# Sample attention units moved by half a stage in a one-core decoder-trunk kernel, with the block of the new values last in each unit's sum

## The chip, the core and the metric

The kernel runs on one core of one Trainium2 chip, as one program. The metric is the device time of one execution in microseconds (us); lower is better. Before the change it is 2066.39 us, the median of 3 runs (2065.44 to 2069.13).

## The reference

One inference step of a small decoder trunk, on a prompt of 512 tokens and on 8 samples of 8 new tokens each, in float32, width 1024. Layer 1 is a convolution module and a gated feed-forward block (FFN). Layer 2 is attention with 16 heads of 64 in three dilation groups (windows 128, 512 and 2048, dilations 1, 4 and 16) and another FFN. Keys and values are shared between the groups' queries as in the lines below; the samples attend to a cache of 1024 earlier rows and to their own new rows.

```python
h, st = conv_module(x, ...);  x = x + h                    # layer 1
x = x + swiglu(x, ...)
k, v = shared_kv(x, pos, kv_norm, w_kv, k_norm)            # layer 2: 3 groups, 16 heads
q = queries(x, pos, b_norm, w_q, q_norm)
for g in range(3):                                         # prompt: band_attention
    kg, vg, valid = gather_keys(cache_g, k[:, :, g], v[:, :, g], r_g, W_g // r_g)
    o_g, lse_g = gathered_attention(q[:, :, g], kg, vg, valid)      # samples
x = x + merge_groups(outs, lses, w_o)                      # softmax over the groups' lse
x = x + swiglu(x, ...)
```

## The kernel before

The work runs in this order: convolution layer, FFN 0, attention, merge (the projection with `w_o`), FFN 1. Two blocks of the convolution are done on VectorE. Every float32 product of the projections is three TensorE matmuls (`mm3`, lines 228 to 230) on operands that ScalarE and VectorE split into a high and a low half. TensorE is busy almost without a break outside the attention.

The attention has two parts.

*The projection stages.* `stage(s)` for s = 0 to 3 computes queries, keys and values of four heads (256 columns, `CW`) in 9 chunks: kind 0 (queries), 1 (keys), 2 (values), each for three dilation groups g. A chunk is a generator with 5 yields, so a stage has 45 steps. At the yields the weight slice `whi`, `wlo` for a later chunk is loaded (`wraw`, 1024 KB) and split. Queries and keys are normed and rotated; the samples' part of them is put into `Qz[s % 2]` and `KN[s]` by `new_keys`, five ticks (about one chunk) after its chunk. Finished rows go to DRAM: `scr` for the prompt, `scs` for the samples' new keys and values, both by `store`, also five ticks later.

*The prompt phase.* `prompt()` does the band attention of the 512 prompt tokens, two heads at a time (8 pairs p), in 88 steps. Per pair it reads back three `nat` tiles of 512 KB (queries and keys), three `v` tiles of 256 KB, and exchanges softmax statistics through DRAM (`sx`, `ot`, `scc`, `cb`).

*The samples' attention* is cut into 8 units u; unit u serves stage s = u // 2 and four of the eight samples. It has steps at whole numbers i relative to its base step 12 + 32 u (`LEAD + u * PERIOD + i`):

- i = -12 to 12: nine loads of old keys, tile `kk` (512 KB each, five buffers; some are issued as two halves);
- i = 0 to 25: TensorE transposes of these tiles into `tp` (line 964), copied by ScalarE to `kt`;
- i = 14, 26, 29: scores, TensorE on `tp` (line 989), the last of them with `KN[s]`, and VectorE's masked maximum; i = 31 to 33 the exponentials;
- i = 33 to 55: ten loads of values, tile `vv` (four buffers), each 8 steps ahead of its use: nine of 512 KB from the cache, and one (ti = 1) of three small transfers from `scs`, the new values;
- i = 37 to 43: transposes of the probabilities; i = 41 to 63: the sum over ten value blocks in the PSUM tile `pv` (line 1062); i = 65 to 67: the result goes to `as`.

Call i up to 31 the first half of a unit and i from 32 the second half. The units overlap: the second half of u runs beside the first half of u + 1, 32 steps later. There are 304 sample steps in all.

`weave` merges two generators: it always runs the one that is behind in its share, so both end together. Before, stage 0 is woven with 33 empty steps and then 12 sample steps, the stages 1 to 3 with 64 sample steps each (`WIN`), and the prompt phase with the 100 that are left.

All these DMAs are issued by one queue, SyncE's (SP), in program order. The order is written out by hand in this sense: the instructions stand on each engine as the woven generators emit them.

Of the kernel before, what the change touches and what calls it, by code (L numbers as in the profile page):

```python
# [90 lines left out]
def trunk(ctx: ExitStack, tc: tile.TileContext, I, O, dbg=None):  # L91
    nc = tc.nc
# [778 lines left out]
    def attention(as_):  # L871
# [26 lines left out]
        def rows2(b, kind, c0):  # L898
            return ck[1][b, :, kind, c0:c0 + CW].rearrange("(j p) c -> p j c", p=128)

        def load3(t, b, kind, c0, q0, q1):
            v = ck[2][b, :, kind, c0:c0 + CW].rearrange("(j q t) c -> t j q c", q=8, t=2)
            for i in range(2):
                nc.sync.dma_start(t[64 * i:64 * i + 64], v[i, :, q0:q1])

        def kk():
            return sm.tile([128, 4, CW], F32, tag="kk", name="kk", bufs=5)

        KN = {}
        PERIOD, LEAD = 32, 12  # L910
        WIN = (64, 64, 64)
        steps = {}

# [16 lines left out]
        pvt = sps.tile([128, CW], F32, name="pv")  # L930

        def sample_unit(u):
# [5 lines left out]
            def at(i, order=1):  # L938
                def put(f):
                    steps.setdefault(LEAD + u * PERIOD + i, []).append((order, f))  # L940
                    return f
                return put


            for n in range(9):
                g, bi = (1 + n // 4, n % 4) if n < 8 else (0, 0)
                b = 4 * ub + bi

                @at(3 * n - 12, 2)
                def _(n=n, g=g, b=b):  # L950
                    t = Z["k", n] = kk()
                    if g == 0:
                        nc.sync.dma_start(t, ck[0][4 * ub:4 * ub + 4, :, 0, c0:c0 + CW].rearrange("b p c -> p b c"))
                    elif g == 1:
                        nc.sync.dma_start(t, rows2(b, 0, c0))
                    else:
                        load3(t, b, 0, c0, 0, 4)
# [74 lines left out]
                        nc.scalar.activation(ph[:w, a:z], pt[:w, a - tl[0]:z - tl[0]], AF.Copy)  # L1032


            for ti in range(10):
                t0 = 41 + 5 * ti // 2

                @at(t0 - 8, 2)
                def _(ti=ti):
                    v = Z["v", ti] = sm.tile([128, 4, CW], F32, tag="vv", name="vv", bufs=4)  # L1040
                    bs = slice(4 * ub, 4 * ub + 4)
                    if ti == 0:
                        nc.sync.dma_start(v, ck[0][bs, :, 1, c0:c0 + CW].rearrange("b p c -> p b c"))
                    elif ti == 1:
                        for g in range(G):
                            nc.sync.dma_start(v[T * g:T * g + T], scs[2][g][32 * ub:32 * ub + 32, c0:c0 + CW]
                                              .rearrange("(b t) c -> t b c", t=T))
                    elif ti < 6:
                        nc.sync.dma_start(v, ck[1][bs, 128 * (ti - 2):128 * (ti - 1), 1, c0:c0 + CW]
                                          .rearrange("b p c -> p b c"))  # L1050
                    else:
                        vb = ck[2][bs, :, 1, c0:c0 + CW].rearrange("b (j q t) c -> t q j b c", q=8, t=2)
                        for t in range(2):
                            nc.sync.dma_start(v[64 * t:64 * t + 64], vb[t, ti - 6])

                @at(t0, 0)
                def _(ti=ti):
                    ph, v = Z["ph"], Z.pop(("v", ti))
                    n = 24 if ti == 1 else 128
                    for bi in range(4):  # L1060
                        r = slice(32 * bi, 32 * bi + 32)
                        nc.tensor.matmul(pvt[r], ph[:n, ti, r], v[:n, bi], start=ti == 0, stop=ti == 9)  # L1062

            @at(65, 0)
            def _():
# [19 lines left out]
        NSAMPLE = max(steps) + 1  # L1085

        def sample_steps():
            for i in range(NSAMPLE):
                for _, f in sorted(steps.get(i, []), key=lambda x: x[0]):
                    f()  # L1090
                yield


        def weave(*gens):

            live = [[g, n, 0] for g, n in gens]
            while live:
                live.sort(key=lambda x: (x[2] + 1) / x[1])
                x = live[0]
                try:  # L1100
                    next(x[0])
                    x[2] += 1
                except StopIteration:
                    live.remove(x)
# [16 lines left out]
        def nat_load(p, g):  # L1121

            t = NAT[p, g] = pnat.tile([128, 8, 128], F32, tag="nat", name="nat", bufs=2)
            nc.sync.dma_start(t, scr[g, :2, :, :, p * 128:p * 128 + 128].rearrange("k r j c -> j (k r) c"))

        with xp:
# [116 lines left out]
            def stage(s):  # L1243
                for kind in range(3):
                    for g in range(G):
                        yield from chunk(s, kind, g)
# [5 lines left out]
                                  scs[kind][g].rearrange("(b t) c -> b t c", t=T))  # L1252

            samples = sample_steps()
            def first_loads():
                yield from range(45 - LEAD)
                yield from islice(samples, LEAD)

            weave((stage(0), 45), (first_loads(), 45))
            for s in range(1, NSTAGE):  # L1260
                if s == NSTAGE - 1:
                    for g in range(2):
# [7 lines left out]
        with ExitStack() as px:  # L1270
# [12 lines left out]
            def both(m):  # L1283

                return (2 * m, 2 * m + 1)

            def nat_transpose(p, i):
                g, k = divmod(i, 2)
                t = NAT[p, g][:, 4 * k:4 * k + 4]
                pt = ps.tile([128, 512], F32, tag="tpp", name="tpp", bufs=2)  # L1290
                for r in range(4):
                    x = pt[:, r * 128:(r + 1) * 128]
                    if g == 0:

                        x = pt.rearrange("p (i r jj) -> p r i jj", i=4, r=4)[:, r]
                    nc.tensor.transpose(x, t[:, r], ident)
                d = QK[p, k, g] = pa.tile([128, 512], F32, tag="qk", name="qk", bufs=6)
                nc.scalar.activation(d, pt, AF.Copy)
# [50 lines left out]
            def do_exp(n):  # L1349
                p, lay, e, j = unit(n)  # L1350
                nb, P = NBS.pop(n), PP[n]
                for ii in range(2):
                    c = cols_of(n, ii)
                    nc.scalar.activation(P[:, ii, c], P[:, ii, c], AF.Exp, scale=SC, bias=nb[:, ii:ii + 1],
                                         accum_out=ST[p][:, lay, 2 * j + ii, e, 1:2])
# [92 lines left out]
            NM = NU // 2  # L1448

            def prompt():  # L1450
                for i in range(5):
                    yield
                for i in range(2):
                    nat_transpose(0, i)
                nat_load(0, 2)
                yield
                for m in range(NM + 9):
                    p, k = divmod(m, 4)
                    if 0 <= m - 1 < NM:
                        for n in both(m - 1):  # L1460
                            do_max(n)
                    if 0 <= m - 3 < NM:
                        do_values(m - 3)
                    yield
                    if 0 <= m - 2 < NM:
                        for n in both(m - 2):
                            do_transpose(n)
                    if m < NM:
                        do_scores(m)
                    if 0 <= m - 1 < NM:  # L1470
                        for n in both(m - 1):
                            do_exp(n)

                    q = p + k // 2
                    if k < 3 and q < NP:
                        for i in (2 * k + 2, 2 * k + 3) if k < 2 else (0, 1):
                            nat_transpose(q, i)
                    if k < 3 and p + 1 < NP:
                        nat_load(p + 1, k)
                    if p < NP:  # L1480
                        if k == 0:
                            v_load(p, 0)
                        elif k == 2:
                            v_load(p, 1)
                            v_load(p, 2)
                        elif k == 3 and 1 <= p < 4:
                            new_rows(1, p - 1)
                            new_rows(2, p - 1)
                    for d, f in ((5, exchange), (6, exchanged), (8, coefficients), (9, coefficients_out), (10, coefficients_in),
                                 (12, combine)):  # L1490
                        if (m - d) % 4 == 0 and 0 <= (m - d) // 4 < NP:
                            f((m - d) // 4)
                    yield

            weave((prompt(), 2 * NM + 24), (samples, NSAMPLE - LEAD - sum(WIN)))
        cx.close()
        return ap

# [97 lines left out]
```

## Time and profile before

| | |
|---|---|
| median of 3 runs | 2066.39 us (2065.44 to 2069.13) |
| profiled execution: its time, its span | 2061.0 us, 2059.1 us |
| mean granted TensorE clock | 0.98 |
| busy: TensorE, VectorE, ScalarE, GpSimd | 1950.8, 1013.1, 810.7, 159.9 us |
| DMA | 387.81 MB, 188 GB/s on average |

"PE" is TensorE's matmuls, "PEld" its weight loads, "DVE" VectorE, "ACT" ScalarE, "POOL" GpSimd, "SPq" the issue of DMAs on SP. A table of windows gives for each stretch of time its length, each engine's busy time with the number of instructions, the granted TensorE clock (1.00 is full), the mean busy share of the core's 16 DMA engines, and the GB/s that they moved. Times in a timeline or a chain are microseconds from the start of the span.

### The profile page before, as it was taken

The page shows a single profiled execution, that of the slowest core. Times are in us where ns is not written, and L with a number is a line of the kernel's source. Part 1 is how long each engine was busy: PE and PEld are TensorE (multiplying, and loading weights), DVE is VectorE, ACT ScalarE, POOL GpSimd, SP SyncE. Part 2 cuts the span into 40 slices and gives each one's busy share as a digit, 9 for nine tenths or more (in the row PEclk, how much of TensorE's full clock was granted, in tenths as well). Part 3 has the DMA queues.
Part 4 walks back from the last instruction along what each step waited for, and adds up shares of the span by engine and source line. Part 5 has one row for each costly group of instructions (what it writes and reads, how often), then busy time and mean ns, then how long its engine had stood idle before and what let it go on. Part 6 is the DMA issues. An engine that isn't in the chain of part 4 may idle for free.

```text
span 2059.1 us, 40751 instructions
## 1 busy us (share of the span) xinstructions
PE 1950.8 (95%) x17109; PEld 1801.3 (87%) x17109; DVE 1013.1 (49%) x1922; ACT 810.7 (39%) x1836; POOL 159.9 (8%) x292
## 2 busy tenths in 40 slices
PE   6989799999999999999999999988897999999999
PEld 6767499999999999998888888866566999999998
DVE  5776665432444486564455356325454454324432
ACT  6554633221222343444344344266564332112221
POOL 1000000000000033130122032000112000000000
PEclk9999899999999999999999999989898999999999
DMA  7430196568655856759778887699979555643222
GB/s 211 144 143 22 34 322 224 197 213 292 204 197 189 290 165 198 212 171 259 209 212 230 246 230 211 205 227 220 205 160 249 202 203 197 217 117 82 76 71 75
DMA packets 368873, 387.81 MB, mean 188 GB/s; under 512 B 17983, under 2 KB 357975, under 8 KB 367010
## 3 DMA queue, kind: packets, MB, share of 16 engines
q1 hardware_dynamic: 368130, 384.06, 62.4%
q8 instruction: 135, 2.21, 0.5%
q0 software_dynamic: 560, 1.14, 0.2%
q14 instruction: 48, 0.39, 0.1%
HBM read 348.07 MB, written 146.86 MB: 240 GB/s over the span
## 4 chain that ended last, share of the span: by engine, by line
PE 84%; DMA 6%; ACT 5%; DVE 3%; SPq 1%; issue 1%; another core or an unknown queue 0%; ACTq 0%; DVEq 0%
PE pmm L230 13%; PE pmm L229 13%; PE pmm L228 13%; PE pj L228 7%; PE pj L229 7%; PE pj L230 7%; PE pj L1191 3%; PE tp L964 3%; PE acc L558 3%; PE pmp L229 2%; PE pmp L230 2%; PE pmp L228 2%; DMA nat<-scr 2%; PE pv L1062 2%; PE tp L989 2%; DMA vv<-in_cache_kv_w_dram 1%
## 5 line engine op out<-in xcount | busy, mean ns | idle before, releaser
L230 PE MATMUL pmm<-uh,wlo 128*128 128x288 f32 x1344 | 396.2, 295 | 0.0
L228 PE MATMUL pmm<-uh,whi 128*128 128x288 f32 x1344 | 395.9, 295 | 0.0
L229 PE MATMUL pmm<-ul,whi 128*128 128x288 f32 x1344 | 395.7, 294 | 0.0
L228 PE MATMUL pj<-whi,xh 128*128 128x256 f32 x1152 | 332.0, 288 | 0.9 <-DVE xT L810 0.9
L229 PE MATMUL pj<-wlo,xh 128*128 128x256 f32 x1152 | 322.3, 280 | 0.0
L230 PE MATMUL pj<-whi,xl 128*128 128x256 f32 x1152 | 322.1, 280 | 0.0
L228 PEld LDWEIGHTS pmm<-uh,whi 128*128 128x128 f32 x1344 | 252.1, 188 | 0.1
L229 PEld LDWEIGHTS pmm<-ul,whi 128*128 128x128 f32 x1344 | 252.1, 188 | 0.1
L230 PEld LDWEIGHTS pmm<-uh,wlo 128*128 128x128 f32 x1344 | 252.1, 188 | 0.0
L228 PEld LDWEIGHTS pj<-whi,xh 128*128 128x128 f32 x1152 | 217.2, 189 | 10.3 <-issue 9.5
L140 ACT ACTIVATE whi<-wraw 128x1024 fp32r<-128x1024 f32 (+3 forms) x206 | 169.2, 872 | 123.0 <-PE pmm L229 100.6
L229 PEld LDWEIGHTS pj<-wlo,xh 128*128 128x128 f32 x1152 | 217.2, 189 | 0.0
L230 PEld LDWEIGHTS pj<-whi,xl 128*128 128x128 f32 x1152 | 216.7, 188 | 0.0
L141 DVE TENSOR_TENSOR wlo<-wraw,whi 128x1024 fp32r<-128x1024 f32 (+3 forms) x206 | 197.7, 1003 | 23.3 <-ACT whi L140 23.0
L228 PE MATMUL pmm<-hh,whi 128*128 128x288 f32 x704 | 207.6, 295 | 0.0
L230 PE MATMUL pmm<-hh,wlo 128*128 128x288 f32 x704 | 207.5, 295 | 0.0
L229 PE MATMUL pmm<-hl,whi 128*128 128x288 f32 x704 | 207.2, 294 | 0.0
L799 DVE TENSOR_TENSOR gt<-pmm,rs 128x576 f32<-128x576 f32 x42 | 31.8, 757 | 224.6 <-PE pmm L230 224.6
L271 ACT ACTIVATE hh<-gt 128x576 fp32r<-128x576 f32 x44 | 30.2, 686 | 263.3 <-DVE gt L800 263.3
L229 PEld LDWEIGHTS pmm<-hl,whi 128*128 128x128 f32 x704 | 132.1, 188 | 0.0
L228 PEld LDWEIGHTS pmm<-hh,whi 128*128 128x128 f32 x704 | 132.1, 188 | 0.0
L230 PEld LDWEIGHTS pmm<-hh,wlo 128*128 128x128 f32 x704 | 132.0, 188 | 0.0
(295 smaller groups left out, 3518.3 us busy)
## 6 DMA issues: line engine op xcount, KB each, us to landing
out_dram<-in_cache_kv_w_dram SPq DMA_DIRECT2D x64, 1016.0 KB
wraw<-in_w_gate_up_dram SPq DMA_DIRECT2D x88, 512.0 KB
out_dram<-in_cache_kv_w_dram SPq DMA_DIRECT2D x32, 1008.0 KB
wraw<-in_w_kv_dram SPq DMA_DIRECT2D x24, 1024.0 KB
wraw<-in_w_down_dram SPq DMA_DIRECT2D x32, 704.0 KB
kk<-in_cache_kv_w_dram SPq DMA_DIRECT2D x40, 512.0 KB
vv<-in_cache_kv_w_dram SPq DMA_DIRECT2D x40, 512.0 KB
scr<-r SPq DMA_DIRECT2D x36, 512.0 KB
```

Source lines behind the costliest of these rows:

```text
L140: nc.scalar.activation(hi[:, c], raw[:, c], AF.Copy)
L141: wstate["lo"].tensor_sub(lo[:, c], raw[:, c], hi[:, c].bitcast(F32))
L228: nc.tensor.matmul(out, wh, xh, start=start, stop=False)
L229: nc.tensor.matmul(out, wh, xl, start=False, stop=False)
L230: nc.tensor.matmul(out, wl, xh, start=False, stop=stop)
L271: nc.scalar.activation(hi, x, AF.Copy)
L558: nc.tensor.matmul(acc[r][32 * (j - m):32 * (j - m) + 32], DG[c][g, j], exf[c][g, j:S + j], start=m == 0, stop=j + 4 >= TAPS)
L799: nc.vector.tensor_mul(halves(t2), pu, halves(rs))
L964: nc.tensor.transpose(pt[:, j * 128:(j + 1) * 128], Z["k", n][:, j, i * 128:(i + 1) * 128], ident)
L989: nc.tensor.matmul(pt[32 * bi:32 * bi + 32, a:a + n], q[:, x, i, b], kn[:, x, i, T * b:T * b + T] if k is None else k[:, i, bi], start=i = ...
L1062: nc.tensor.matmul(pvt[r], ph[:n, ti, r], v[:n, bi], start=ti == 0, stop=ti == 9)
L1191: nc.tensor.matmul(pt[:, :CW], xs[:, k], x[:, k], start=k == 0 and x is wh, stop=k == KT - 1 and x is wl)
```

## The change

Three edits:

1. Stage 0 is woven with 64 steps (20 empty ones, then the first 44 sample steps) instead of 45 (33 empty, then 12). `EARLY` = 44 replaces `LEAD` = 12 in the two places that count how many sample steps are used before stage 1. So every sample step comes 32 steps, one `PERIOD`, earlier relative to the stages: the first half of unit u = 2s now runs in stage s itself, beside the projections of its own heads, and no longer in stage s + 1.
2. The prompt phase is woven with 304 - 44 - 192 = 68 sample steps instead of 100.
3. The ten value blocks of a unit are taken in the order 0, 2, 3, ..., 9, 1 instead of 0 to 9. So the load of the new values (ti = 1) still stands behind the stores to `scs` of its own stage in program order. `start` and `stop` of the sum in `pv` follow the position i.

```diff
-        PERIOD, LEAD = 32, 12
+
+        PERIOD, LEAD, EARLY = 32, 12, 44
...
-            for ti in range(10):
-                t0 = 41 + 5 * ti // 2
+            for i, ti in enumerate((0, 2, 3, 4, 5, 6, 7, 8, 9, 1)):
+                t0 = 41 + 5 * i // 2
...
-                        nc.tensor.matmul(pvt[r], ph[:n, ti, r], v[:n, bi], start=ti == 0, stop=ti == 9)
+                        nc.tensor.matmul(pvt[r], ph[:n, ti, r], v[:n, bi], start=i == 0, stop=i == 9)
...
-            def first_loads():
-                yield from range(45 - LEAD)
-                yield from islice(samples, LEAD)
-
-            weave((stage(0), 45), (first_loads(), 45))
+            def first_steps():
+                yield from range(64 - EARLY)
+                yield from islice(samples, EARLY)
+
+            weave((stage(0), 45), (first_steps(), 64))
...
-            weave((prompt(), 2 * NM + 24), (samples, NSAMPLE - LEAD - sum(WIN)))
+            weave((prompt(), 2 * NM + 24), (samples, NSAMPLE - EARLY - sum(WIN)))
```

How the instructions move, at three places. First the SP queue in the middle of stage 0 (`wraw` are weights, `tbl` rotation tables, `scr`, `scs` and `out_dram` the stores of finished chunks, `kk` old keys). Before:

```order
L1229 DMA scr<-r_7383 128x4x256
L122 DMA wraw<-in_w_kv_dram 128x8x256
L1135 DMA tbl<-tabs 128x640
L1229 DMA scr<-r_7564 128x4x256
L122 DMA wraw<-in_w_kv_dram 128x8x256
L1135 DMA tbl<-tabs 128x640
L1228 DMA scs_3225<-r_7745 64x256
L1229 DMA scr<-r_7745 128x4x256
```

The same stretch with the change:

```order
L956 DMA kk<-in_cache_kv_w_dram 128x4x256
L1230 DMA scr<-r_7383 128x4x256
L122 DMA wraw<-in_w_kv_dram 128x8x256
L956 DMA kk<-in_cache_kv_w_dram 128x4x256 x2
L1136 DMA tbl<-tabs 128x640
L1230 DMA scr<-r_7564 128x4x256
L122 DMA wraw<-in_w_kv_dram 128x8x256
L956 DMA kk<-in_cache_kv_w_dram 128x4x256
L904 DMA kk<-in_cache_kv_w_dram 64x4x256 x2
L1136 DMA tbl<-tabs 128x640
L1229 DMA scs_3225<-r_7747 64x256
L1230 DMA scr<-r_7747 128x4x256
```

The first five key loads of unit 0 now stand here, between the weight loads of stage 0; before, the first `kk` stood four weight loads further on.

Second, the SP queue at the very end of the prompt phase (`sx`, `ot`, `scc`, `cb` are the exchange of softmax statistics, `vv` the samples' values, `v` the prompt's values). Before:

```order
L1304 DMA v<-scr 128x4x128 x2
L1366 DMA ot<-sx 128x16
L1398 DMA cb<-scc 64x1024 x2
L1049 DMA vv<-in_cache_kv_w_dram 128x4x256
L1054 DMA vv<-in_cache_kv_w_dram 64x4x256 x4
L1362 DMA sx<-st 32x4x4 x4
L1392 DMA scc<-ct 16x128
L1054 DMA vv<-in_cache_kv_w_dram 64x4x256 x2
L1366 DMA ot<-sx 128x16
L1398 DMA cb<-scc 64x1024 x2
L1054 DMA vv<-in_cache_kv_w_dram 64x4x256 x2
```

With the change:

```order
L1305 DMA v<-scr 128x4x128 x2
L1367 DMA ot<-sx 128x16
L1399 DMA cb<-scc 64x1024 x2
L1055 DMA vv<-in_cache_kv_w_dram 64x4x256 x2
L1047 DMA vv<-scs_3228 8x4x256
L1047 DMA vv<-scs_3229 8x4x256
L1047 DMA vv<-scs_3230 8x4x256
L1363 DMA sx<-st 32x4x4 x4
L1393 DMA scc<-ct 16x128
L1367 DMA ot<-sx 128x16
L1399 DMA cb<-scc 64x1024 x2
```

After the last `v` loads five big value loads were still to come, two of them behind the last pair's `sx` stores; now it is one, and the three small loads of new values, all ahead of `sx`.

Third, TensorE at the same place, up to the first matmul of the merge (`po` and `tpt` are the prompt's, `tpc` transposes the merge coefficients of a pair, `pv` is a sample's sum, `tp<-mf,osb` its result). Before:

```order
L1062 MATMUL pv<-vv,ph 32x256 x4
L1417 MATMUL tpt<-ident,P 128x128 x8
L1389 MATMUL tpc<-ident,cf 16x128
L1439 MATMUL po<-pts,v 64x128 x8
L1062 MATMUL pv<-vv,ph 32x256 x12
L1389 MATMUL tpc<-ident,cf 16x128
L1062 MATMUL pv<-vv,ph 32x256 x8
L1075 MATMUL tp<-mf,osb 128x32 x2
L228 MATMUL pmp<-oh,whi 128x288
```

With the change:

```order
L1063 MATMUL pv<-vv,ph 32x256 x4
L1418 MATMUL tpt<-ident,P 128x128 x8
L1390 MATMUL tpc<-ident,cf 16x128
L1440 MATMUL po<-pts,v 64x128 x8
L1063 MATMUL pv<-vv,ph 32x256 x8
L1390 MATMUL tpc<-ident,cf 16x128
L1063 MATMUL pv<-vv,ph 32x256 x4
L1076 MATMUL tp<-mf,osb 128x32 x2
L228 MATMUL pmp<-oh,whi 128x288
```

Behind the prompt's last `po` stood five value blocks of the last sample unit; now three stand there.

More of the change, by code (lines that the diff above doesn't have):

```diff
@@ L1056, in _ @@
                 @at(t0, 0)
-                def _(ti=ti):
+                def _(ti=ti, i=i):
                     ph, v = Z["ph"], Z.pop(("v", ti))
```

## The prediction

> **What bounds the kernel now.** I read the windows first, cut at the ends of the stages. These ends come from the chain of waits, in which the last chunk of each stage closes with its samples' matmuls (line 1191), and the merge begins with `oh`:
>
> ```profile
> 834.91 1.89 PE pj L1191 x16
> 992.65 2.02 PE pj L1191 x16
> 1164.50 2.02 PE pj L1191 x16
> 1334.92 2.04 PE pj L1191 x16
> 1573.91 0.64 ACT oh L271
> ```
>
> ```profile
> 718.00:836.80 118.80, 118.80 (x1006) 117.57 (x1006) 85.08 (x177) 48.05 (x123) 34.09 (x64) 1.00 0.61 192
> 836.80:994.60 157.80, 155.21 (x1447) 142.61 (x1446) 86.83 (x188) 70.19 (x165) 29.45 (x60) 1.00 0.72 209
> 994.60:1166.50 171.90, 165.81 (x1547) 148.03 (x1546) 87.79 (x191) 73.11 (x173) 29.46 (x60) 0.99 0.80 228
> 1166.50:1337.00 170.50, 164.41 (x1548) 146.63 (x1547) 86.88 (x185) 71.78 (x167) 29.37 (x58) 1.00 0.75 215
> 1337.00:1573.00 236.00, 192.63 (x1925) 138.53 (x1923) 100.86 (x440) 141.87 (x427) 26.38 (x21) 0.91 0.93 198
> ```
>
> Columns: length, then PE, PEld, DVE, ACT, POOL busy, PE clock, DMA share, GB/s. The rows are the stages 0 to 3 and the prompt phase. In the stages PE is busy 96 to 100% of the time and the DMA share is 0.61 to 0.80: these are bound by TensorE. The prompt phase is the other way round: PE 82%, at a lowered clock, and the 16 DMA engines 0.93 busy on average. Everything before 718 and after 1600 us is untouched by the change.
>
> Second, who does what where: the sum `pv` alone, in the same five windows, counts the second halves of units (80 matmuls each):
>
> ```profile
> 718.00:837.00 119.00, 0.00 (x0) 0.00 (x0) 0.00 (x0) 1.00 0.61 192
> 837.00:995.00 158.00, 6.38 (x80) 1.57 (x80) 0.00 (x0) 1.00 0.72 210
> 995.00:1167.00 172.00, 12.77 (x160) 3.14 (x160) 0.95 (x2) 0.99 0.80 228
> 1167.00:1337.00 170.00, 12.77 (x160) 3.14 (x160) 0.95 (x2) 1.00 0.75 215
> 1337.00:1573.00 236.00, 21.61 (x240) 5.06 (x240) 1.91 (x4) 0.91 0.93 198
> ```
>
> So stage 1 has one second half, stages 2 and 3 two each, the prompt phase three. First halves stand 0, 2, 2, 2 and 2, by the step table.
>
> Third, the DMA of the prompt phase (1337 to 1573 us): the packets of the SP queue with their share, then its largest issues, line by line; and the same queue row for stage 2 (995 to 1167 us):
>
> ```profile
> q1 hardware_dynamic: 66995, 46.29, 92.0%
> ...
> nat<-scr SPq DMA_DIRECT2D x22, 512.0 KB
> vv<-in_cache_kv_w_dram SPq DMA_DIRECT2D x15, 512.0 KB
> vv<-in_cache_kv_w_dram SPq DMA_DIRECT2D x24, 256.0 KB
> kk<-in_cache_kv_w_dram SPq DMA_DIRECT2D x16, 256.0 KB
> v<-scr SPq DMA_DIRECT2D x16, 256.0 KB
> cb<-scc SPq DMA_DIRECT2D x16, 256.0 KB
> kk<-in_cache_kv_w_dram SPq DMA_DIRECT2D x6, 512.0 KB
> ```
>
> ```profile
> q1 hardware_dynamic: 39473, 39.03, 79.8%
> ```
>
> The phase loads 27 `vv` tiles (15 + 24 / 2) and 14 `kk` tiles (6 + 16 / 2), 41 in all. A packet holds an engine 0.92 x 236 x 16 / 66995 = 51.9 ns here, and 0.798 x 172 x 16 / 39473 = 55.6 ns in stage 2, although here the mean packet is 0.69 KB and there 0.99 KB. The time goes by packets more than by bytes.
>
> Fourth, the chain over 1335 to 1580 us by line:
>
> ```profile
> by line: DMA nat<-scr 13.9%; DMA vv<-in_cache_kv_w_dram 11.9%; DMA v<-scr 11.4%; PE po L1439 6.0%; PE tpt L1417 5.2%; PE sc L1327 4.8%; ACT P L1354 4.8%; PE tpp L1296 4.2%; DMA ot<-sx 3.5%; PE tp L964 3.3%; PE pv L1062 3.1%; DMA sx<-st 2.6%
> ```
>
> Transfers hold 43% of it, most of them the prompt's own `nat` and `v`, which share the queue with the samples' loads.
>
> **The change part by part.** By the step table, stage 0 gains one first half (with nine `kk` loads), stage 1 one second half (nine `vv` loads from the cache and the three small ones), stages 2 and 3 keep two of each, and the prompt phase loses one second and one first half. The shift is exactly one period of 32 steps, so inside the stages the pattern only changes which unit is in which place.
>
> *Stage 1* becomes what stages 2 and 3 are now: (171.9 + 170.5) / 2 - 157.8 = +13.4 us. By PE's busy time alone it would be 165.1 - 155.2 = +9.9.
>
> *Stage 0* gains a first half. Stage 1 is stage 0 plus two first halves and one second: (157.8 - 118.8 - 13.4) / 2 = +12.8 us; by busy time (155.2 - 118.8 - 9.9) / 2 = +13.3. ScalarE (48 of 118.8 us) and VectorE (85) have room for its copies. The nine `kk` loads stand in the SP queue ahead of later weight loads. At a DMA share of 0.61 I cost them at nothing more; if they hold up `wraw`, the price is half of what PE idles in stage 2, 6.1 / 2 = 3 us. What unit 0 needs from its own stage is early enough: the scores with `KN[0]` come at step 61 of 64, that is 42.9 of the stage's 45, the last `new_keys` at about 35.
>
> Together the stages get longer by 26.2 us, bounds 23.2 (busy time only) and 29.
>
> *The prompt phase* loses 18 of its 41 loads: 18 x 512 packets of 1 KB = 9216, or 9.44 MB. Without a trace of the lighter phase, the ends are these. By packets at 51.9 ns it is 29.9 us of all 16 engines, at 55.6 ns 32.0 us. By bytes, 9.44 / 46.29 of 217 us busy gives 44.3. At the peak that this trace shows just behind the phase, 350 GB/s, it is 27.0:
>
> ```profile
> 1580.00:1590.00 10.00, 10.00 (x76) 10.00 (x75) 6.11 (x11) 2.68 (x4) 0.81 (x1) 0.98 0.98 350
> ```
>
> By PE's work alone (the 23.2 of above) it is 23. I take 32.0, because the 1 KB packets of stage 2 are the nearest row to what is removed and the share of 0.93 says that the transfers set the pace. The Trainium skill, "DMA: Bandwidth & Descriptors", section "Specifications", gives HBM's limit per core as about 358 GB/s; by that an estimate is 26.4 us for the 9.44 MB, and the sum below would be about nothing instead of a gain. The trace agrees with that limit outside the phase (350), but within it the engines are 0.93 busy at 198 GB/s, so here the measured packets decide.
>
> *The tail.* The last value load is now issued behind the last pair's exchange:
>
> ```profile
> 1553.07 5.18 SPq L1362 DMA_DIRECT2D sx<-st  x4
> 1562.37 0.35 SPq L1366 DMA_DIRECT2D ot<-sx  x1
> 1563.97 1.29 SPq L1054 DMA_DIRECT2D vv<-in_cache_kv_w_dram  x2
> 1568.33 0.37 PE L1389 MATMUL tpc<-ident,cf 128*16 128x128 f32 x1 [5.99 <-DVE cf L1385]
> 1570.82 1.08 PE L1062 MATMUL pv<-vv,ph 128*32 128x256 f32 x8 [1.10 <-DMA vv<-in_cache_kv_w_dram]
> ```
>
> With the change it stands ahead of `sx`, so `pv` can end with `tpc`, 2.5 us sooner; what is late next is the exchange itself (`sx` to `tpc`). If `sx` is also no longer held 5.2 us in the queue, up to 5 us more. I take 2.
>
> *The new order of blocks* moves three 32 KB loads from second to last place. Eight steps of lead hide them; uncovered they would cost once, at the last unit, less than the 6.9 us that a far larger load took above from its issue (1563.97) to `pv` (1570.82).
>
> Sum: 26.2 - 32.0 - 2 = -7.8, say -8 us. The profiled execution took 2061.0 us (span 2059.1), which becomes 2053. It lies 5.4 us under the median of the runs, 2066.4, which becomes 2058.4.
>
> **The rivals.**
> (a) *Bytes, not packets.* If the phase follows bytes, it loses 44 us: 26 - 44 - 2 = -20, 2046. For it: the phase is nearly all DMA. Against it: the two packet times above, and PE needs 192.6 - 23 = 169 us plus ends.
> (b) *Peak rate.* The removed loads would have cost only 27 us of room: 26.2 - 27.0 - 0 = -1, 2065.5. The skill's page above names that limit.
> (c) *Slower: the prompt's transfers wait on latency, not on a queue.* Then only the samples' own links leave the chain: `vv` 11.9% of 245 us x 18/41 = 12.8, `pv` 3.1% x 80/240 = 2.5, `tp` L964 3.3% x 1/2 = 4.0, together 19.3 us. 26.2 - 19.3 = +7, 2073. It decides where the phase shrinks by less than 26 us. For it: `nat` has two buffers, and SP waits for their release:
>
> ```profile
> SPq L1124 <- PE tpp L1296: 20.3, 6, 6.0
> ```
>
> Against it: a release comes late because PE is late, and PE waits for transfers that are queued.
>
> **How the numbers follow.** A difference of 0.2%, 4.1 us, is about what a measurement of this kernel tells from no change. Forecast 0.50 (from -13 to -3: of it 0.45 beyond 0.2%), (a) 0.13, (b) 0.19 (0.15 within), (c) 0.18 (0.16 beyond). Faster 0.45 + 0.13 + 0.02 = 0.60; same 0.05 + 0.15 + 0.02 = 0.22; slower 0.18. The range goes from 2047, most of the way to (a), to 2071, most of the way to (c); the forecast's own range is 2053 to 2064.
>
> **What would show it.** Right: stage 0 about 131 us, stage 1 about 171 and like stages 2 and 3; `pv` counts of 0, 160, 160, 160, 160; about 57,800 packets in a prompt phase of some 202 us with the DMA share still near 0.9; the last `pv` just behind `tpc`. Wrong: a prompt phase above 210 us, with a DMA share that has fallen (c), or below 195 (a); PE idle in stage 0 behind `whi`, which would put the nine key loads on the path; or PE waiting for `KN[0]` or `vv<-scs`.

## The result, and the profile after

The changed kernel takes 2049.94 us (median of 4 runs, 2048.85 to 2050.89), the kernel before 2067.57 (4 runs, 2065.44 to 2069.13). The ratio is 0.9915, with a 95% interval of 0.9898 to 0.9932: 17.6 us faster, against the 8 that were forecast. The time lies inside the range on record (2047 to 2071), near its lower end, but below the forecast's own range (2053 to 2064): it is nearer to the time of rival (a), 2046, than to 2058. In a later repetition of the changed kernel one execution of six took 2721.16 us at a mean granted clock of 0.65; it is left out of every figure here.

The profiled execution of the change took 2048.85 us, with a span of 2047.1. That is only 12 us less than the profiled execution of before. The page's rows:

```profile
span 2047.1 us, 40767 instructions
PE 1948.9 (95%) x17109; PEld 1799.7 (88%) x17109; DVE 1013.2 (49%) x1922; ACT 810.2 (40%) x1836; POOL 158.8 (8%) x292
```

TensorE does the same 17109 matmuls in the same busy time (1950.8 before). So the gain is for the most part TensorE's idle time, which fell by 10 us. To see where, read the chain of waits at the last matmuls of the first chunk of stage 0 and of the last chunk of each stage (line 1191, now 1192), and at the first `oh` of the merge. Before, and then with the change:

```profile
727.18 1.81 PE pj L1191 x16
```

```profile
731.46 1.88 PE pj L1192 x16
853.68 1.89 PE pj L1192 x16
1021.77 2.09 PE pj L1192 x16
1192.24 2.09 PE pj L1192 x16
1362.71 2.11 PE pj L1192 x16
1561.58 0.64 ACT oh L271
```

With the rows of before that the prediction shows, the pieces are:

| piece | before | after | difference |
|---|---|---|---|
| up to the first chunk of stage 0 | 727.2 | 731.5 | +4.3 |
| stage 0, from there | 107.7 | 122.2 | +14.5 |
| stage 1 | 157.7 | 168.1 | +10.4 |
| stage 2 | 171.9 | 170.5 | -1.4 |
| stage 3 | 170.4 | 170.5 | 0 |
| prompt phase | 239.0 | 198.9 | -40.1 |

The first row belongs to work that the change does not touch: in the other profiles read below, six of them of altered kernels of before, the same sums start between 730.1 and 732.9, so the profiled execution of before was an early one. Without this row the pieces sum to -16.6, near the 17.6 of the medians. The window of the prompt phase before, up to the first `oh`, and then the windows of the change, same columns as in the prediction:

```profile
1337.00:1573.90 236.90, 193.19 (x1926) 138.96 (x1924) 100.86 (x440) 142.09 (x428) 26.38 (x21) 0.91 0.93 198
```

```profile
722.30:855.60 133.30, 132.56 (x1171) 127.90 (x1171) 85.56 (x185) 57.72 (x141) 31.61 (x64) 1.00 0.67 203
855.60:1023.90 168.30, 163.82 (x1542) 146.15 (x1541) 87.43 (x190) 72.88 (x172) 29.40 (x60) 1.00 0.85 228
1023.90:1194.30 170.40, 164.32 (x1546) 146.54 (x1545) 87.80 (x191) 72.99 (x173) 29.39 (x60) 1.00 0.85 230
1194.30:1364.80 170.50, 164.42 (x1547) 146.63 (x1546) 86.89 (x185) 71.70 (x167) 29.30 (x58) 1.00 0.81 215
1364.80:1561.60 196.80, 168.65 (x1665) 125.51 (x1662) 100.80 (x430) 129.55 (x404) 23.29 (x19) 0.92 0.79 188
```

Stage 0 is still filled by TensorE (132.6 of 133.3 us). In the prompt phase the DMA share has fallen from 0.93 to 0.79. TensorE's busy time there fell by 24.5 us (193.2 to 168.7) and its idle time by 15.6. The sum `pv` alone in five windows of the change, the four stages and the prompt phase, has the counts that the prediction named: 0, 160, 160, 160, 160.

```profile
722.30:855.60 133.30, 0.00 (x0) 0.00 (x0) 0.00 (x0) 1.00 0.67 203
855.60:1023.90 168.30, 12.77 (x160) 3.14 (x160) 0.48 (x1) 1.00 0.85 228
1023.90:1194.30 170.40, 12.77 (x160) 3.14 (x160) 0.95 (x2) 1.00 0.85 230
1194.30:1364.80 170.50, 12.77 (x160) 3.14 (x160) 0.95 (x2) 1.00 0.81 215
1364.80:1561.60 196.80, 13.01 (x160) 3.28 (x160) 1.43 (x3) 0.92 0.79 188
```

The chain of waits through the prompt phase, by line, no longer leads with transfers. Before (from 1337.0 to 1573.9 us; the prediction shows a slightly longer stretch), and then with the change:

```profile
by line: DMA nat<-scr 14.3%; DMA vv<-in_cache_kv_w_dram 12.3%; DMA v<-scr 11.7%; PE po L1439 6.2%; PE tpt L1417 5.4%; PE sc L1327 5.0%; ACT P L1354 5.0%; PE tpp L1296 4.4%; DMA ot<-sx 3.7%; PE tp L964 3.4%; PE pv L1062 3.2%; DMA sx<-st 2.7%
```

```profile
by line: PE sc L1328 12.2%; PE po L1440 11.1%; PE tpp L1297 10.1%; PE tpt L1418 9.1%; DMA v<-scr 7.5%; DMA nat<-scr 5.5%; PE pv L1063 3.7%; ACT P L1355 3.4%; DMA cb<-scc 3.1%; ACT qk L1299 3.0%; PE tp L965 2.9%; issue 2.8%; DMA vv<-scs 2.6%
```

### The profile page after: what moved, and what is told of

Its sections match the earlier page's. It is cut to its first block, busy times and chain, and to the rows that moved or that the text cites. A ratio compares the mean times of both kernels' runs of the same rounds, so it can differ in the third digit from the quotient of the medians.

```text
span 2047.1 us, 40767 instructions
## 1 busy us (share of the span) xinstructions
PE 1948.9 (95%) x17109; PEld 1799.7 (88%) x17109; DVE 1013.2 (49%) x1922; ACT 810.2 (40%) x1836; POOL 158.8 (8%) x292
## 4 chain that ended last, share of the span: by engine, by line
PE 88%; ACT 4%; DVE 3%; DMA 3%; issue 1%; SPq 1%; another core or an unknown queue 0%; ACTq 0%; DVEq 0%
PE pmm L230 13%; PE pmm L229 13%; PE pmm L228 13%; PE pj L228 7%; PE pj L229 7%; PE pj L230 7%; PE pj L1192 3%; PE tp L965 3%; PE acc L558 3%; PE pmp L229 2%; PE pmp L230 2%; PE pmp L228 2%; PE pv L1063 2%; PE tp L990 2%; ACT prod L588 1%; PE sc L1328 1%
```

## Experiments

From here on, "phase" is the time from the end of stage 3 to the first `oh`: 237.0 us before, 196.8 with the change (the last row of the table counts from the start of stage 3's last sums, 2 us earlier). A phase length is read from one profiled execution of each kernel, so it carries the scatter of single executions. In the windows quoted below the first number behind the times is its length.

**Loads alone.** In the kernel before:

```diff
+                    if u == 7:      # key loads
+                        Z["k", n] = <a view of Qz[0]>; return
...
+                    if u == 5 and ti != 1:      # value loads
+                        Z["v", ti] = <a view of Qz[0]>; return
```

> The kernel before, but 18 of the 41 sample loads of the prompt phase are left out (the nine cache value loads of unit 5 and the nine key loads of unit 7; the matmuls read a tile that is there already), with all compute kept. Theory A (packets of the transfers set the steady part of the phase): -30 us, the whole of the 30.6 us that the phase lost ahead of its tail. Theory B (transfers and TensorE take turns on the path, so each counts only for its own share): about -15 us, the fall of PE's idle time.

Measured: ratio 0.9891 (0.9873 to 0.9910), 22 us less (19 to 26); the phase is 211.1 us, 25.9 less.

```profile
1339.30:1550.40 211.10, 181.89 (x1926) 131.66 (x1924) 99.21 (x440) 141.41 (x429) 26.41 (x21) 0.96 0.79 177
```

It lies between the two theories. Of the 25.9 us, 11.3 are TensorE's busy time, although its 1926 matmuls are all still there: they took 193.2 us before at a granted clock of 0.91, and take 181.9 here at 0.96. The DMA queue's rows of this phase, of the phase before and of the phase with the change:

```profile
q1 hardware_dynamic: 57440, 37.11, 78.3%
```

```profile
q1 hardware_dynamic: 67063, 46.53, 92.0%
```

```profile
q1 hardware_dynamic: 57216, 36.65, 78.4%
```

Without the 18 loads the queue holds the engines 0.783 x 211.1 = 165 us, against 0.920 x 236.9 = 218 before: 53 us less engine time for 26 us less time. A packet holds an engine for 46.0 ns on average in it (0.783 x 211.1 x 16 / 57440), 52 before and 43.1 with the change. The run with the old order of the blocks, below, is the cleanest comparison: its phase of 193.6 us has the same packets and bytes as the change's.

```profile
q1 hardware_dynamic: 57216, 36.65, 87.7%
```

There they hold the engines for 170 us (0.877 x 193.6), 47.5 ns each, against 154 us with the change, in a phase that is 3 us shorter. So the engines' busy time is not a measure of the work in the queue, and a price per packet that is taken from it is not a constant. That the difference is waiting inside the engines is likely, but no row shows it.

**Compute alone.** In the kernel before, unit 7 gets no steps below i = 41 but its loads and no transposes of its probabilities, and uses unit 6's; unit 5 sums two blocks of ten.

```diff
+                    if u == 7 and order < 2 and i < 41:
+                        return f
...
+                    if u == 7:
+                        Z["ph"], Z["st"] = ZU[6]["ph"], ZU[6]["st"]
...
-                    for bi in range(4):
+                    for bi in range(4 if u != 5 or ti in (0, 9) else 0):
```

> The kernel before, but compute of about one sample unit is left out of the prompt phase (unit 7's transposes, scores and exponentials, 8 of 10 blocks of unit 5's sum; unit 7 uses unit 6's probabilities), with every load kept. Theory A: 0 to -5 us, since the loads still set the pace. Theory B: -15 to -20 us, TensorE's own time for them.

Measured: 0.9966 (0.9955 to 0.9977), 7 us less; the phase is 230.5 us, 6.5 less, for 13.6 us less of TensorE's busy time.

```profile
1342.20:1572.70 230.50, 179.55 (x1685) 129.33 (x1683) 97.02 (x431) 131.51 (x405) 26.32 (x21) 0.87 0.93 203
```

While the loads are there they set most of the pace: the DMA share stays at 0.93, and half of the compute time that is left out is filled with waiting again. Theory A is nearer, though not at zero.

**Both.** The two edits together.

> The kernel before with both left out of the prompt phase: the nine value loads of unit 5 and the nine key loads of unit 7, and the compute of about one unit (8 of 10 blocks of unit 5's sum, unit 7's transposes, scores and exponentials). If the two savings add (22.5 + 7 us): -30 us, prompt phase 204 us. If compute is worth more once the loads no longer set the pace: -36 to -40 us, phase 194 to 198, near the 197 of the changed kernel, and nothing is left for the tail.

Measured: 0.9835 (0.9811 to 0.9860), 34 us less; the phase is 205.5 us, 31.5 less.

```profile
1340.10:1545.60 205.50, 169.13 (x1684) 123.02 (x1682) 96.05 (x431) 130.21 (x404) 26.35 (x21) 0.92 0.80 182
```

In the phase the two savings add (25.9 + 6.5 = 32.4), as in the first of the two expectations. With nearly the loads and the compute of the changed kernel's phase, it is still 8.7 us longer than that phase. The next part finds them at the end of the phase.

**The end of the phase.** The prompt's last `po` and the first `oh` of the kernel before (the rows between them, with the last value load at 1563.97 and its sum at 1570.82, stand in the prediction), and then SP's issues and TensorE's sums there with the change, in order of time (start, length):

```profile
1556.67 1.37 PE L1439 MATMUL po<-pts,v 128*64 128x128 f32 x16
1573.91 0.63 ACT L271 ACTIVATE oh<-ap 128x512 fp32r<-128x512 f32 x1
```

```profile
1543.94 1.29 SPq L1055 DMA_DIRECT2D vv<-in_cache_kv_w_dram  x2
1546.83 4.29 SPq L1363 DMA_DIRECT2D sx<-st  x4
1554.52 1.37 PE L1440 MATMUL po<-pts,v 128*64 128x128 f32 x16
1558.75 0.27 PE L1390 MATMUL tpc<-ident,cf 128*16 128x128 f32 x1 [1.86 <-DVE cf L1386]
1558.95 0.63 PE L1063 MATMUL pv<-vv,ph 24*32 24x256 f32 x8
1561.58 0.63 ACT L271 ACTIVATE oh<-ap 128x512 fp32r<-128x512 f32 x1
```

From the end of the prompt's last `po` to the merge it was 15.9 us (1558.0 to 1573.9) and is 5.7 (1555.9 to 1561.6): 10.2 us less. This is the tail. The last big value load is now issued 10 us ahead of that `po`, and no longer 6 us behind its end.

The same two rows in the run with both left out, where the queue is as light but the steps are woven as before:

```profile
1528.22 1.37 PE L1450 MATMUL po<-pts,v 128*64 128x128 f32 x16
1545.60 0.63 ACT L271 ACTIVATE oh<-ap 128x512 fp32r<-128x512 f32 x1
```

Its tail is 16.0 us (1529.6 to 1545.6), as before; with the loads alone left out it is 16.7. Ahead of the tail its phase takes 189.5 us, the change's 191.1, the kernel's before 221.1. So the 8.7 us lie in the tail (10.3 longer there, 1.6 shorter ahead of it), and a lighter queue alone does not shorten it. Two runs move the loads at the end.

In the changed kernel, the last two big value loads of the last unit later:

```diff
-                @at(t0 - 8, 2)
+                @at(t0 - (2 if u == 2 * NSTAGE - 1 and ti in (8, 9) else 8), 2)
```

> The changed kernel, with the last two big value loads of the last unit issued 2 instead of 8 steps ahead, so that the last stands behind the last pair's exchange in the SP queue, as before the change. If the tail's gain of 9.5 us came from that order: the kernel loses 5 to 9 us of its 17, -9 to -12 us against the kernel before. If not: -15 to -17 us.

Measured: 0.9929 (0.9916 to 0.9943), 14.7 us less than before. The unaltered change, repeated beside it:

> The changed kernel again, beside the others of this call: -15 to -18 us, with the prompt phase at 197 us in the profile.

Measured: 0.9911 (0.9895 to 0.9927), 18.4 us less; its phase was not read. So the late loads cost about 4 us, hardly clear of the scatter and less than the 5 to 9 that were expected if the order were all. The profile with the late loads:

```profile
1551.34 1.37 PE L1440 MATMUL po<-pts,v 128*64 128x128 f32 x16
1554.30 1.29 SPq L1055 DMA_DIRECT2D vv<-in_cache_kv_w_dram  x2
1560.32 1.08 PE L1063 MATMUL pv<-vv,ph 128*32 128x256 f32 x8 [7.05 <-DMA vv<-in_cache_kv_w_dram]
1564.73 0.63 ACT L271 ACTIVATE oh<-ap 128x512 fp32r<-128x512 f32 x1
```

The tail is back at 12.0 us (1552.7 to 1564.7), with TensorE waiting 7.05 us for the load. But the `po` ends 3 us earlier in the phase than with the change, so of 6.3 us in the tail 3.3 remain in the phase (200.1 against 196.8).

In the kernel before, the last unit's value loads earlier:

```diff
-                @at(t0 - 8, 2)
+                @at(t0 - (14 if u == 2 * NSTAGE - 1 and ti > 4 else 8), 2)
...
-                    v = Z["v", ti] = sm.tile(...)
+                    v = Z["v", ti] = kk() if u == 2 * NSTAGE - 1 and ti % 2 else sm.tile(...)
```

> The kernel before, with the last five value loads of the last unit issued 14 instead of 8 steps ahead, so that all stand ahead of the last pair's exchange in the SP queue (every second value tile of that unit uses a free key buffer). If the tail's gain came from that order in the queue: -5 to -9 us. If the tail follows the load in the phase and not the order: -2 us or less.

Measured: 0.9999 (0.9984 to 1.0013), nothing.

```profile
1564.93 0.69 PE L1440 MATMUL po<-pts,v 128*64 128x128 f32 x4 [8.87 <-DMA v<-scr]
1570.80 1.63 PE L1440 MATMUL po<-pts,v 128*64 128x128 f32 x16
1578.44 0.63 ACT L271 ACTIVATE oh<-ap 128x512 fp32r<-128x512 f32 x1
```

The tail is 6.0 us here as well (1572.4 to 1578.4). But TensorE waits 8.87 us for the prompt's `v`, now behind the sample's loads, and the last `po` ends 10 us later in the phase than before. In this crowded queue the order only decided who waits. So a gain at the tail needs both: the loads ahead of the exchange, and a queue with room for them.

The loads do not stand ahead because of the new order of the blocks. In the changed kernel with the old order in the last units (below), a 512 KB block is the last one again, and the tail is just as short, 5.6 us (1554.0 to 1559.6):

```profile
1552.65 1.37 PE L1440 MATMUL po<-pts,v 128*64 128x128 f32 x16
1559.59 0.63 ACT L271 ACTIVATE oh<-ap 128x512 fp32r<-128x512 f32 x1
```

And the kernel before with the new order alone has a tail of 14.9 us. What remains is the weaving: 68 sample steps instead of 100 stand beside the prompt's 88, so a lead of eight steps is 10.4 of the prompt's steps and no longer 7.0. No run changes that number alone.

**The order of the blocks alone.**

```diff
-        PERIOD, LEAD, EARLY = 32, 12, 44
+        PERIOD, LEAD, EARLY = 32, 12, 12      # with the order 0, 2, ..., 9, 1 and stage 0 as before
```

> The kernel before with only the order of the value blocks changed (0, 2 to 9, 1); the steps are not moved. If the move of 32 steps is all that counts: 0, at most -2 us, since the last value block of the last unit is now the small one. If the new order itself brings part of the 17 us: -4 us or more.

Measured: 1.0037 (1.0025 to 1.0049), 7 us slower; the phase is 245.7 us, 8.7 more.

```profile
1341.00:1586.70 245.70, 192.43 (x1926) 138.97 (x1924) 98.68 (x440) 141.97 (x429) 26.44 (x21) 0.90 0.88 189
```

Neither value that was expected. The loss lies ahead of the tail. The same order in unit 5 alone:

> The kernel before with the new order in unit 5 alone, whose value loads open the prompt phase. If the 6.5 us of the order alone come from there (big value loads 2.5 steps earlier, onto the phase's first nat and v loads): +5 to +8 us. If they come from the end of the phase: 0 to +2 us.

Measured: 1.0006 (0.9991 to 1.0022); the phase is 239.8 us. Most of the 7 us does not come from that unit; from which it comes is open. The opposite, in the changed kernel:

```diff
-            for i, ti in enumerate((0, 2, 3, 4, 5, 6, 7, 8, 9, 1)):
+            for i, ti in enumerate((0, 2, 3, 4, 5, 6, 7, 8, 9, 1) if u in (0, 2, 4) else range(10)):
```

> The changed kernel with the old order of the value blocks in units 1, 3, 5, 6 and 7, where their new values are stored early enough; only units 0, 2 and 4 keep the new order. If the new order costs what it did alone (6 to 8 us): -23 to -26 us. If it costs that only while the phase is saturated: -16 to -19 us, as the change.

Measured: 0.9894 (0.9869 to 0.9919), an interval that overlaps the change's own (0.9898 to 0.9932). The phase is 193.6 against 196.8 us, one profile each. Whether the order still costs something in the lighter phase is not settled.

**Fewer and more steps moved.** `EARLY` = 28 and 52 in place of 44, and 52 with the old order in the odd units.

> Half of the shift: 28 sample steps in stage 0 instead of 44, so 84 are left for the prompt phase. If what the prompt phase loses is proportional to the steps moved: -8 us. If the first steps that leave the saturated phase are worth more: -10 to -14 us.

> More of the shift: 52 sample steps in stage 0, so 60 are left for the prompt phase. If the loads still set the pace of the phase: -19 to -21 us. If the transfers no longer do (their share is 0.79 after the change): -15 to -18 us, as after the change, since the eight steps then cost in the stages what they save in the phase.

> 52 sample steps in stage 0 with the old order in the odd units. If the order costs time in the lighter phase too: -30 us or more. If not: -25 to -28 us, as with 52 steps alone.

Measured: 28 steps 0.9945 (0.9930 to 0.9960), 11 us less; 52 steps 0.9870 (0.9855 to 0.9885), 27 us less; 52 with the old order 0.9882 (0.9858 to 0.9906), not told apart from 52 alone. 52 steps is the fastest version with all its work, 2041.13 us. The windows of 28 steps (stages 2 and 3, phase), then of 52 (stage 0, stage 1, phase):

```profile
1014.20:1190.50 176.30, 168.84 (x1548) 150.90 (x1551) 87.91 (x191) 73.14 (x173) 27.98 (x60) 0.97 0.80 220
1190.50:1364.90 174.40, 167.24 (x1549) 149.26 (x1550) 86.89 (x185) 71.94 (x167) 28.48 (x58) 0.98 0.78 217
1364.90:1570.10 205.20, 171.74 (x1829) 126.07 (x1828) 97.47 (x436) 133.78 (x411) 23.19 (x19) 0.96 0.90 198
```

```profile
718.80:859.90 141.10, 138.34 (x1226) 133.30 (x1227) 88.11 (x190) 64.47 (x154) 33.75 (x64) 1.00 0.71 210
859.90:1031.60 171.70, 165.84 (x1546) 147.51 (x1545) 87.79 (x191) 72.73 (x173) 29.63 (x60) 0.99 0.85 222
1373.90:1552.70 178.80, 157.73 (x1635) 115.03 (x1633) 96.70 (x428) 125.27 (x393) 23.33 (x19) 0.96 0.81 189
```

A shift by half a period gives the phase 32 us (237.0 to 205.2), but stages 2 and 3 each take 4 to 6 us more than the 170.5 of the change, which spends part of it. Most of this extra is TensorE's busy time for about as many matmuls, at a clock of 0.97 and 0.98 (168.8 and 167.2 us, against 164.3 and 164.4 at 1.00); why the clock is lower there is open. Eight steps more than the change give the phase another 18 us (196.8 to 178.8), for 9 us more in the stages. So the phase gives 32, 8 and 18 us for the first 16 steps, the next 16 and the next 8, which is no simple rule, and both expectations for 52 steps were too small. Of the 18 us, 11 are TensorE's busy time (168.7 to 157.7, with 30 matmuls fewer, the clock at 0.96 and no longer 0.92) and 7 its idle time (28 to 21). The DMA share stays at about 0.8, so it does not tell whether more can be gained; why these eight steps give so much is open.

## Why the prediction was right, and where it was not

*The stages.* +26.2 us was forecast from the lengths of the stages, with 23.2 from busy time as the lower bound; the rows give +23.5. Stage 1 came out at 168.1, not 171.2, so there the busy price (9.9) was nearer than the length (13.4): the waits of stages 2 and 3 did not all come with the work. Stage 0 (here the time from its first chunk on) paid 14.5 for 12.8. The nine key loads ahead of the weights held up nothing much: TensorE idles 0.7 us in it.

*The loads.* The forecast took 32.0 us, by packets at 55.6 ns, and gave the compute that leaves the phase no price beside it. Up to the last `po` the phase lost 30.0 us, so the term looks right, but that is luck: two errors cancel. Loads alone give 25.9, close to the 27.0 that 350 GB/s would give. Compute adds 6 more. The packet price was the step that failed: it took the engines' busy share for work, and the two phases with the same 57216 packets show that it is not (170 and 154 us of engine time). The sign named for it failed too: the packets came out as said (57216), but the DMA share is 0.79 and not near 0.9. How much of the missing 6 us is the price, and how much that the lighter phase waits on other things, is open. By the limit of about 358 GB/s in the Trainium skill, "DMA: Bandwidth & Descriptors", section "Specifications", the estimate was 26.4 us; the run without loads comes close to it (25.9 us in its profile, 22 by the medians' ratio), although the phase as a whole moves only 177 to 198 GB/s. Rival (b) had this price, but not the compute and the tail beside it.

*The tail.* This is the term that was mis-sized: 2 us taken, "up to 5 us more" left open, 10.2 measured. The prediction counted that `pv` would end with `tpc`, which it does (1558.75 and 1558.95), but not that the whole exchange of the last pair would be issued earlier against the prompt's last `po`. Before, the four `sx` stores were issued from 1553.07 to 1558.25, into the end of that `po`; now they are out at 1551.1, 3 us before it begins. Taken alone in the kernel before, early loads gave nothing, and a lighter queue alone left the tail at 16 us, so the gain belongs to the two together.

*The order of the blocks* was priced at nothing. Alone it costs 7 us. The cover named for it, eight steps of lead, protects the block that is moved; eight of the other nine move forward by two or three steps, and the prediction did not ask what these pass in the queue. Whether the cost remains in the changed kernel is not settled, and its mechanism is open.

*The rivals.* (a), 20 us by bytes, is close in size to the 17.6 but not as a mechanism, since loads alone give 26 us and not 44. (c), slower, falls: the waits on `nat` and `v`, which it took to be latency and kept, shrank from 26.0% of a chain of 237 us (62 us) to 13.0% of 197 us (26 us). Its own sum also had a slip: the share of `vv` alone is cut by 18 of 41 loads, though 9 of the 27 `vv` leave; by these it would be 9.7 us and not 12.8, and the rival +10 and not +7.

Together: +23.5 in the stages, -30.0 up to the last `po`, -10.2 behind it, -16.6 in all, and 17.6 by the medians. Against the forecast's +26.2, -32.0 and -2, the errors in the stages and in the loads nearly cancel (2.7 less, 2.0 less), and the tail's 8.2 us is nearly the whole of what the sum missed.

## What to carry to other kernels

Where one phase is held mostly by its transfers and the ones before it by TensorE, work that has loads of its own can gain by moving forward. Try more than one shift: here eight steps beyond the change gave another 9 us, and neither the DMA share nor the step table told so beforehand. Do not price a removed load by the busy share of a crowded phase; here the rate that the trace of before shows just behind the phase, 350 GB/s, came close, and a share of the compute that went with the loads had to be added. Read the end of a phase by itself: what stands in the queue behind its last exchange was paid in full there, and issuing it earlier helped only together with a queue that had room.

## What the runs showed of the hardware

The mean time that a packet holds a DMA engine is not a constant of its size. The same 57216 packets (36.65 MB) held one for 43.1 ns each in the phase of the change, and for 47.5 ns when the blocks of five units stood in the old order, in a phase that was 3 us shorter (193.6 against 196.8). Before the change it was 52 ns at a share of 0.92, and 46.0 with 18 loads fewer at 0.78. Leaving out these 14% of the packets took 24% off the engines' busy time (218 to 165 us) and 11% off the phase.

TensorE's busy time for the same matmuls depends on what else the phase does: 1926 of them took 193.2 us at a granted clock of 0.91, and 181.9 us at 0.96 with the 18 loads left out.
